# The first stage of an encoder trunk: projections from x * w with rstd at the readout, and all engines in written order

## The chip, the cores and the metric

The kernel runs on one core of a Trainium2 chip. The metric is the device time of one launch in microseconds (us); the median of three runs before is 2257.11 us. TensorE (PE) does the matmuls, VectorE (DVE), ScalarE (ACT) and GpSimd (POOL) the elementwise work; SyncE (SP) and, here and there, ACT issue the transfers (DMAs). PE writes PSUM, eight banks of 128 x 512 fp32; DVE and ACT read and write it too.

## The reference

One encoder layer runs over a prompt of 1024 tokens and a sample of 256 tokens, with a width of 1024, all fp32. The change touches only the beginning of the token-mixing block:

```python
def rmsnorm(x, w):
    y = xf * lax.rsqrt(jnp.mean(xf * xf, -1, keepdims=True) + EPS)
    return y * w
...
h = rmsnorm(x, norm_mix_w)
proj = h @ w_in          # columns: q/k/v, ab, gate, sg_u (512), sg_v (512), two branch gates
...
def spatial_gating_branch(u, v, ln_w, ln_b, w_s, b_s):
    u = gelu(u)
    v = layernorm(gelu(v), ln_w, ln_b)
    mixed = einsum('gts,bnsgc->bntgc', w_s, v) + b_s      # chunks of 128 tokens, 4 groups
    return u * mixed
```

After it come the gated DeltaNet branch, the branch merge, cross-attention into 256 memory tokens, a SwiGLU feed-forward part and a last norm.

## The kernel before

**Tiles.** Tokens lie in three blocks, `BLOCKS`: prompt blocks 0 and 1 of 512 tokens each and block 2, the sample, of 256. x is held with its 1024 features as 8 pieces (k) of 128 partitions and the tokens along the free axis. Every fp32 product is made of three fp32r matmuls: an operand is split into a high part, an ACT copy with rounding, and a low part, source minus high part (`split`: the copy on ACT, the subtraction on the engine that is named). Per k there is hi*hi, lo*hi and hi*lo. So x becomes `hi{b}`, `lo{b}`, and a weight `whi`, `wlo` (or `svh`, `svl` for the v columns).

**Norm.** `Norm.add` squares on ACT and adds on DVE; the rest sums over the partitions with matmuls against a column of ones, computes rstd with 11 small DVE instructions (`rsqrt` has three Newton steps), broadcasts rstd over the partitions by matmuls with the identity, and then, for each k, one DVE instruction makes x * w * rstd (`nt`) and `split` makes its two parts. `to_h` gives the low part to POOL for even k and to DVE for odd k.

**Stages.** The first stage computes, block by block, `sgv(b)` (the v columns in two halves of 264, tokens as the stationary operand, each token group of 128 with 24 matmuls, followed by `gelu2` on ACT and DVE) and `sgu(g, b)` (u group g of 128 columns, 24 matmuls). The order on PE is: sample's v, `bias()`, sample's u groups 0 and 1; block 0's v, u groups 0 and 1; block 1's v, u groups 0 and 1; then u groups 2 and 3 of all blocks. `ln(cs)` is the layer norm of v, and `mix(g, b, ug)` the spatial mix, which writes to DRAM. Behind this stage come the DeltaNet stage with the remaining projections, and the rest of the layer.

**Order of the work.** PE runs in the order in which the program is written (`manual_schedule` for TensorE). All other engines are ordered by a scheduler with its own cost model. Side work is written as generators (`K.side`): each yields an estimate of PE time in ns after which it wants to go on, and `K.pump` lets it go on when PE's estimated clock is there. `K.until` and `K.finish` push the side work on until it is done. `LAG0` and similar numbers are such estimates. Weights stream through a queue, `K.order`: `K.take` hands out the next split weight, `K.ahead` splits one more and loads the next. The low part of a split weight is made by POOL in this stage.

**Start.** SP issues the sample's x (`xs`), the small vectors `sm` (norm weights among them), two constants, half of the v weights, the rest of the constants; then block 0's x (`x0`) and the other half of the v weights. The sample's norm (`first_norm`) runs while the v weights are split, half 0 by POOL and DVE, half 1 likewise.

Of the kernel before, what the change touches and what calls it, by code (L numbers as in the profile page):

```python
# [8 lines left out]
F32 = mybir.dt.float32  # L9
F32R = mybir.dt.float32r  # L10
# [31 lines left out]
def f32(ap):  # L42
    return ap.bitcast(F32)
# [11 lines left out]
class Trunk:  # L55
# [68 lines left out]
    def split(self, hi, lo, src, eng=None):  # L124
        self.nc.scalar.activation(hi, src, AF.Copy)  # L125
        (eng or self.nc.vector).tensor_tensor(out=lo, in0=src, in1=f32(hi), op=ALU.subtract)  # L126
# [37 lines left out]
def trunk_kernel(ctx: ExitStack, tc: tile.TileContext, a):  # L164
# [52 lines left out]
    def bank(p=pq, tag="b"):  # L217
        return p.tile([P, 512], F32, tag=tag, name="bank")
# [4 lines left out]
    def rsqrt(y, x, scratch):  # L223
        V.tensor_scalar(out=y.bitcast(I32), in0=x.bitcast(I32), scalar1=-0.5, scalar2=float(0x5F3759DF), op0=ALU.mult, op1=ALU.add)
        for _ in range(3):
            V.scalar_tensor_tensor(out=scratch, in0=y, scalar=-0.5, in1=x, op0=ALU.mult, op1=ALU.mult)
            V.tensor_tensor(out=scratch, in0=scratch, in1=y, op=ALU.mult)
            V.scalar_tensor_tensor(out=y, in0=scratch, scalar=1.5, in1=y, op0=ALU.add, op1=ALU.mult)

    class Norm:  # L230


# [62 lines left out]
    def to_h(h, b):  # L295
        return lambda k, t: split(h[b][0][:, k, :], h[b][1][:, k, :], t, V if k % 2 else G)

    def act_tiles(p=None):

        p = p or hp  # L300
        return [
            (
                p.tile([P, KT, n], F32R, tag=f"hi{b}", name=f"hi{b}"),
                p.tile([P, KT, n], F32R, tag=f"lo{b}", name=f"lo{b}"),
            )
            for b, (_, n) in enumerate(BLOCKS)
        ]
# [29 lines left out]
            SY.dma_start(x[:, k : k + 2, :], src[:, k : k + 2, t0 : t0 + n])  # L337
        return x

    def sv_raw(half):  # L340
        raws = [K.raw() for _ in range(2)]
        for i, raw in enumerate(raws):
            SY.dma_start(raw, a["w_sv"][half][:, i * 1056 : (i + 1) * 1056])
        return raws

    def sv_split(half, raws):
        lo = svp.tile([P, 8 * 264], F32R, tag="lo", name="svl")
        hi = svp.tile([P, 8 * 264], F32R, tag="hi", name="svh")
        for i, raw in enumerate(raws):
            sl = slice(i * 1056, (i + 1) * 1056)  # L350
            split(hi[:, sl], lo[:, sl], raw, V if i else G)
        sv.append((hi, lo))


    xs = hp.tile([P, KT, NS], F32, tag="lo1", name="xs")
    for k in range(0, KT, 2):
        SY.dma_start(xs[:, k : k + 2, :], a["xT"][:, k : k + 2, NP:])
    SY.dma_start(sm, a["small"])
    SY.dma_start(cst[:, C_BD:], a["const"][:, C_BD:])
    sv_raw0 = sv_raw(0)  # L360
    SY.dma_start(cst[:, :C_BD], a["const"][:, :C_BD])
    x_h = act_tiles()

    def first_norm():

        nm = Norm(xp, 512)
        for k in range(0, KT, 2):
            nm.add(xs[:, k : k + 2, :].rearrange("p k t -> p (k t)"))
        nm.n = NS
        yield from nm.rest(lambda k: xs[:, k, :], S_MIX, to_h(x_h, 2), 0, lag=0, halves=2)  # L370

    first = K.side(first_norm())
    sv_split(0, sv_raw0)
    x0 = x_load(a["xT"], 0, 512, "x0")
    sv_split(1, sv_raw(1))
    K.finish(first)

    done = set()

    def other_norms():  # L380
        yield from norm(xp, lambda k: x0[:, k, :], 512, S_MIX, to_h(x_h, 0), 600, 0, LAG0)
        done.add(0)
        x1_ = x_load(a["xT"], 512, 512, "x1")
        yield 3000
        yield from norm(xp, lambda k: x1_[:, k, :], 512, S_MIX, to_h(x_h, 1), 900)
        done.add(1)
        mem = x_load(a["memT"], 0, 512, "mem")
        yield 6000
        yield from norm(xp, lambda k: mem[:, k, :], 512, S_MEM, lambda k, t: SY.dma_start(md[k], t))

    norms = K.side(other_norms())


    ybd = dp.tile([HEADS, P, NTOK], F32, name="ybd")
# [31 lines left out]
    bias2 = sp.tile([P, 4, P], F32, name="bias2")  # L426
    SY.dma_start(bias2, a["sg_b"].unsqueeze(0).to_broadcast([P, 4, P]))

    def ln(cs):
# [8 lines left out]
        V.tensor_scalar(out=var[:, cs], in0=var[:, cs], scalar1=1.0 / 512, scalar2=4.0 * EPS, op0=ALU.mult, op1=ALU.add)  # L438
# [56 lines left out]
        V.tensor_copy(gcol.rearrange("p d r -> p (d r)"), pt[:, :80])  # L495

    def sgv(b):
        if b < 2:
            K.until(norms, lambda: b in done)
        for half in (0, 1):  # L500
            w = sv[half]
            nv = 264 if half == 0 else 248
            for c in range(4 * b, min(4 * b + 4, NCH)):
                cs = slice((c % 4) * P, (c % 4 + 1) * P)
                hi, lo = x_h[b]
                ps = bank(pm)
                n = 0
                for k in range(KT):
                    wh, wl = wk(w, k, 264)
                    for l, r in ((hi[:, k, cs], wh), (lo[:, k, cs], wh), (hi[:, k, cs], wl)):  # L510
                        mm(ps[:, :264], l, r, n == 0, n == 23)
                        n += 1
                    yield 0
                acc = (s0 if half == 0 else s1)[:, c : c + 1]
                gelu2(sp, ps[:, :nv], vg[:, c, half * 264 : half * 264 + nv], nv, acc)
                if half:
                    V.tensor_copy(ab[:, c, :], ps[:, 248:264])
        lns[b] = K.side(ln(slice(4 * b, min(4 * b + 4, NCH))))
        K.ahead()

    def bias():
# [6 lines left out]
    def mix(g, b, ug):  # L528
# [11 lines left out]
        V.tensor_tensor(out=ug, in0=ug, in1=mx, op=ALU.mult)  # L540
        SY.dma_start(ybd[g, :, t0 : t0 + n], ug)

    ws, mixes = [], []

    def sgu(g, b):
        t0, n = BLOCKS[b]
        if len(ws) == g:
            ws.append(K.take())
        ps = bank(pm)[:, :n]
        yield from proj(ps, ws[g], x_h, b)  # L550
        if (g, b) in ((0, 2), (0, 1), (2, 2), (3, 2)):
            K.ahead()
        if len(mixes) > 2:
            K.finish(mixes[-3])
        ug = sp.tile([P, 512], F32, tag="ug", name="ug", bufs=3)[:, :n]
        gelu2(sp, ps, ug, n)
        mixes.append(K.side(mix(g, b, ug)))

    for b in (2, 0, 1):
        K.main(sgv(b))  # L560
        if b == 2:
            bias()
        elif b == 1:
            K.side(decays())
        K.main(sgu(0, b))
        K.main(sgu(1, b))
# [1564 lines left out]
```

## Time and profile before

| | us |
|---|---|
| median of 3 runs | 2257.11 (2254.49 to 2257.84) |
| the profiled execution | 2255.0 |
| its span, first to last instruction | 2253.2 |
| PE busy | 2196.2 (97%) |
| DVE busy | 1394.0 (62%) |
| ACT busy | 815.5 (36%) |
| POOL busy | 532.7 (24%) |

The page has 40 slices of 56 us each; the first one is the stage that is changed. A line of the timeline begins with the start in us from the begin of the span and the duration; then come the engine, the line of the kernel, the operation, and what it writes and reads. A number in brackets at the end is how long the engine had been idle before, and what ended that. A group's line ends with its busy time, the mean of one in ns, and the idle time before its instructions. Matmuls overlap, so their pace is the distance of their starts and not their duration.

### The profile page before, as it was taken

The numbers are of one execution on the slowest core, as the hardware profiler recorded it, in microseconds if no ns is written. First come the engines' busy times: TensorE is split into PE (matmuls) and PEld (weight loads), VectorE is DVE, ScalarE is ACT, GpSimd is POOL, SyncE is SP. The second block draws the span as 40 slices with busy tenths as digits, with TensorE's granted clock in tenths as the row PEclk, the third lists the DMA queues.
The fourth block names the chain that finished last, engine by engine and source line by source line (L and its number), as shares of the span: only waits on it lengthen the run. The fifth ranks groups of instructions, "written<-read, shape, count | busy, mean of one in ns | idle before, by whom it ended". The sixth has DMA issues, their size and how long they took to land.

```text
span 2253.2 us, 32407 instructions
## 1 busy us (share of the span) xinstructions
PE 2196.2 (97%) x12468; PEld 1918.3 (85%) x12468; DVE 1394.0 (62%) x2770; ACT 815.5 (36%) x1481; POOL 532.7 (24%) x355
## 2 busy tenths in 40 slices
PE   6999999999999999999999999899999999999998
PEld 6988888888888898888888888688888888888888
DVE  7768788887985964664534537544334334568575
ACT  5434243433424433233343423323232323243453
POOL 3010000000000000013231331565666566300031
PEclk9999999999999999999999999999999999999999
DMA  5221322223234445962231431223222222493531
GB/s 185 83 79 68 104 69 87 77 69 95 73 111 125 159 140 165 305 236 94 84 106 45 157 143 57 75 76 110 87 82 76 88 76 82 136 363 126 198 111 57
DMA packets 191301, 262.47 MB, mean 116 GB/s; under 512 B 72410, under 2 KB 102698, under 8 KB 191146
## 3 DMA queue, kind: packets, MB, share of 16 engines
q1 hardware_dynamic: 171306, 231.30, 30.9%
q10 hardware_dynamic: 19840, 29.11, 3.5%
q8 instruction: 97, 1.59, 0.3%
q14 instruction: 58, 0.48, 0.1%
HBM read 182.19 MB, written 78.16 MB: 116 GB/s over the span
## 4 chain that ended last, share of the span: by engine, by line
PE 82%; DVE 8%; issue 4%; DMA 2%; ACT 2%; POOL 1%; SPq 0%; POOLq 0%; ACTq 0%; DVEq 0%
PE bank L108 81%; PE bank L121 1%; DMA tbd<-stage 1%; DVE acc L599 1%; DVE wlo L126 1%; DMA t<-sgd 1%; DVE nt L284 1%; DVE U L845 0%; DVE sw L903 0%; DVE lo L126 0%; DMA stage<-gtd 0%; DVE W L745 0%; DVE nacc L249 0%; DVE aT L714 0%; DVE zt L837 0%
## 5 line engine op out<-in xcount | busy, mean ns | idle before, releaser
L108 PE MATMUL bank<-hi,whi 128*128 128x512 f32 (+1 forms) x2144 | 763.3, 356 | 2.8 <-ACT whi L125 1.7
L108 PE MATMUL bank<-lo,whi 128*128 128x512 f32 (+1 forms) x2144 | 748.8, 349 | 1.1 <-POOL lo L126 1.1
L108 PE MATMUL bank<-hi,wlo 128*128 128x512 f32 (+1 forms) x2144 | 748.3, 349 | 0.9 <-DVE wlo L126 0.9
L108 PEld LDWEIGHTS bank<-hi,wlo 128*128 128x128 f32 x2144 | 406.0, 189 | 54.9 <-DVE wlo L126 1.3
L108 PEld LDWEIGHTS bank<-hi,whi 128*128 128x128 f32 x2144 | 406.9, 190 | 52.7 <-ACT whi L125 2.2
L108 PEld LDWEIGHTS bank<-lo,whi 128*128 128x128 f32 x2144 | 407.1, 190 | 49.8 <-POOL lo L126 1.4
L126 POOL TENSOR_TENSOR wlo<-raw,whi 128x1024 fp32r<-128x1024 f32 x70 | 177.8, 2542 | 377.2 <-ACT whi L125 377.2
L125 ACT ACTIVATE whi<-raw 128x1024 fp32r<-128x1024 f32 (+1 forms) x141 | 144.5, 1026 | 195.3 <-PE bank L108 146.9
L126 POOL TENSOR_TENSOR wlo<-room,whi 128x1024 fp32r<-128x1024 f32 x42 | 100.6, 2396 | 115.7 <-ACT whi L125 115.7
L108 PE MATMUL bank<-bhl,whi 128*128 128x512 f32 x408 | 125.7, 389 | 0.0
L126 DVE TENSOR_TENSOR wlo<-raw,whi 128x1024 fp32r<-128x1024 f32 (+1 forms) x71 | 82.3, 1159 | 43.6 <-ACT whi L125 41.5
L125 ACT ACTIVATE whi<-room 128x1024 fp32r<-128x1024 f32 x42 | 44.6, 1061 | 142.5 <-PE bank L108 138.6
L1796 DVE TENSOR_TENSOR room<-room,bank 128x512 f32<-128x512 f32 x21 | 14.5, 688 | 131.8 <-ACT room L1567 131.8
L108 PEld LDWEIGHTS bank<-bhl,whi 128*128 128x128 f32 x408 | 76.5, 188 | 15.9
L599 DVE SCALAR_TENSOR_TENSOR acc<-craw,sm,acc 128x510 f32<-128x510 f32 (+1 forms) x96 | 73.6, 766 | 20.5 <-ACT acc L597 19.0
L108 PE MATMUL bank<-bhl,wlo 128*128 128x512 f32 x204 | 79.5, 390 | 1.2 <-DVE wlo L126 1.2
L745 DVE TENSOR_TENSOR W<-W,UT 128x2 f32<-128x2 f32 (+30 forms) x155 | 73.2, 472 | 10.1 <-DMA W<-in_eye 5.8
L248 ACT ACTIVATE nsq<-x 128x512 f32<-128x512 f32 (+1 forms) x70 | 40.2, 583 | 102.7 <-DVE x L1237 92.4
L962 ACT ACTIVATE gs<-bank 128x512 f32<-128x512 f32 (+1 forms) x60 | 31.2, 520 | 125.2 <-PE bank L108 119.9
L1589 DVE SCALAR_TENSOR_TENSOR t<-bank,t 128x512 f32<-128x512 f32 (+1 forms) x44 | 24.6, 558 | 82.2 <-PE bank L108 82.2
L249 DVE TENSOR_TENSOR nacc<-nacc,nsq 128x512 f32<-128x512 f32 (+1 forms) x72 | 54.4, 755 | 33.2 <-ACT nsq L248 31.9
L108 PE MATMUL bank<-bhl,ahl 128*128 128x512 f32 x312 | 73.8, 392 | 0.0
(345 smaller groups left out, 4223.1 us busy)
## 6 DMA issues: line engine op xcount, KB each, us to landing
raw<-in_w_gu SPq DMA_DIRECT2D x44, 512.0 KB, 3.9
braw<-gq SPq DMA_DIRECT2D x14, 1024.0 KB, 5.4
raw<-in_w_g SPq DMA_DIRECT2D x20, 512.0 KB, 3.3
gq<-t SPq DMA_DIRECT2D x33, 256.0 KB, 2.0
gtd<-gs ACTq DMA_DIRECT2D x32, 256.0 KB, 2.0
w<-in_w_dn SPq DMA_DIRECT2D x8, 1024.0 KB, 11.9
raw<-in_w_qkv SPq DMA_DIRECT2D x12, 512.0 KB, 3.6
gq<-r SPq DMA_DIRECT2D x22, 256.0 KB, 4.3
```

The costliest lines, as they stand in the source:

```text
L108: self.nc.tensor.matmul(out, l, r, start=start, stop=stop, skip_group_check=more)
L121: self.nc.tensor.transpose(out, x, ident)
L125: self.nc.scalar.activation(hi, src, AF.Copy)
L126: (eng or self.nc.vector).tensor_tensor(out=lo, in0=src, in1=f32(hi), op=ALU.subtract)
L248: S.activation(sq, x, AF.Square)
L249: (eng or V).tensor_tensor(out=self.acc, in0=self.acc, in1=sq, op=ALU.add)
L284: V.scalar_tensor_tensor(out=t, in0=xk(k), scalar=sm[:, wcol + k : wcol + k + 1], in1=pb[:, :n], op0=ALU.mult, op1=ALU.mult)
L599: V.scalar_tensor_tensor(out=dst, in0=src, scalar=wj, in1=dst, op0=ALU.mult, op1=ALU.add)
L745: V.tensor_tensor(out=t3, in0=u3[:, i:, c:].rearrange("p j c -> p c j"), in1=XL[:, 32 * i + i : 32 * i + 32].unsqueeze(1).to_broadcast([P, ...
L962: S.activation(t, ps, AF.Tanh, scale=0.5)
L1589: V.scalar_tensor_tensor(out=out, in0=u, scalar=sign, in1=t, op0=ALU.mult, op1=ALU.mult)
L1796: V.tensor_tensor(out=c22, in0=c22, in1=pe, op=ALU.add)
```

## The change

The stage's beginning, until block 0's x is normalised, is written out by hand and put under `manual_schedule` for DVE, ACT, POOL and SP as well, so that each engine runs it in the order of the text.

- The sample's v and u (groups 0 and 1) are computed from x * w (`xw`, split by ACT's scaled copy and one DVE instruction) in place of the normalised x. rstd comes in when the product is read: for v as the per-token scale of ACT's square and tanh and, since the layer norm that follows takes a common factor out, in its epsilon (`e2`); for u by a multiply with rstd broadcast over the partitions (`rb2`).
- rstd itself is computed by `rsqrt9`, 8 instructions in place of 10.
- The v weights are split by ACT and DVE alone. POOL gets only the low parts of the first two u weights and of half of block 0's x.
- `sm` and two constants are issued by ACT; the order of SP's transfers is new, and the remaining constants come last.
- Block 0's squares are made between the sample's steps, with sums in PSUM.
- `sgv(0)` takes token groups 0 to 2 together in half 0, so that each k gives nine matmuls in place of three.
- The sample's normalised x (`hi2`, `lo2`), needed by u groups 2 and 3 and the later projections, is made afterwards in `other_norms`, ahead of block 1's norm.

```diff
-    def sv_split(half, raws):
-        ...
-            split(hi[:, sl], lo[:, sl], raw, V if i else G)
...
-        yield from nm.rest(lambda k: xs[:, k, :], S_MIX, to_h(x_h, 2), 0, lag=0, halves=2)
...
+    first_stage.enter_context(tc.manual_schedule(engines={V.engine, S.engine, G.engine, SY.engine}))
...
+    S.dma_start(sm, a["small"])
+    S.dma_start(cst[:, C_BD:], a["const"][:, C_BD:])
+    S.dma_start(ident, a["const"][:, C_ID : C_ID + P])
+    xs_load(0)
+    sv_load(0, 0)
+    for k in (2, 4, 6):
+        xs_load(k)
+    sv_load(0, 1)
+    for i in range(2):
+        sv_load(1, i)
+    SY.dma_start(raw_u[0], a["w_u"][0])
     x0 = x_load(a["xT"], 0, 512, "x0")
+    SY.dma_start(raw_u[1], a["w_u"][1])
...
     def sgv(b):
...
+        for half, cs in ((0, (0, 1, 2)), (0, (3,)), (1, (0,)), ...) if b == 0 else [(half, (c,)) for half in (0, 1) for c in range(4)]:
...
+    def xw_split(*ks):
+        w = lambda k: sm[:, S_MIX + k : S_MIX + k + 1]
+        for k in ks:
+            S.activation(xw[:, 0, k, :], xs[:, k, :], AF.Copy, scale=w(k))
+        for k in ks:
+            V.scalar_tensor_tensor(out=xw[:, 1, k, :], in0=xs[:, k, :], scalar=w(k), in1=f32(xw[:, 0, k, :]), op0=ALU.mult, op1=ALU.subtract)
...
+    xw_split(0, 1)
+    square2(0)
+    sv_split(0, 0)
+    xw_split(2, 3)
+    xw_split(4, 5)
+    xw_split(6, 7)
+    sv_split(0, 1)
+    for k in (2, 4, 6):
+        square2(k)
+    sv_split(1, 0)
+    for k0 in (0, 4):
+        for i in range(2):
+            sgv2(0, k0, i)
...
+    rsqrt9(y2, ms, sc, e2)
...
+    sv_split(1, 1)
+    K.split_w(0)
+    square0(0, 1)
+    gelus = [gelu_pair(half) for half in range(2)]
+    next(gelus[0])
+    square0(2, 3)
+    for _ in gelus[0]:
+        pass
+    sgv2(1, 0, 0)
+    sgv2(1, 0, 1)
+    sgv2(1, 4, 0)
...
+    sgv2(1, 4, 1)
+    rb2 = raw_u[0][:, :NS]
+    S.activation(rb2, pb2[:, :NS], AF.Copy)
+    square0(4, 5)
+    next(gelus[1])
+    K.split_w(1)
+    square0(6, 7)
+    for _ in gelus[1]:
+        pass
+    pu = sgu2(0, range(KT))
+    ugs = [sgu2_out(0, pu)]
+    pu = sgu2(1, range(4))
...
+    rsqrt9(y0, ms, sc, h0)
+    sgu2(1, range(4, 8), pu)
+    ugs.append(sgu2_out(1, pu))
...
+    bias()
...
+    for k in range(KT):
+        t = sq_tile()
+        V.scalar_tensor_tensor(out=t, in0=x0[:, k, :], scalar=sm[:, S_MIX + k : S_MIX + k + 1], in1=pb0, op0=ALU.mult, op1=ALU.mult)
+        to_h(x_h, 0)(k, t)
+    first_stage.close()
...
+    def other_norms():
+        x1_ = x_load(a["xT"], 512, 512, "x1")
+        yield NORM2
+        for k in range(KT):
+            ...
+            to_h(x_h, 2)(k, t)
+            yield 600
+        x_h[1] = ...
+        yield from norm(xp, lambda k: x1_[:, k, :], 512, S_MIX, to_h(x_h, 1), 900)
...
-        if (g, b) in ((0, 2), (0, 1), (2, 2), (3, 2)):
+        if (g, b) in ((0, 1), (2, 2), (3, 2)):
             K.ahead()
...
-    for b in (2, 0, 1):
+    for b in (0, 1):
         K.main(sgv(b))
...
-LAG0, LAGF, LAGF2, PACEF = 7500, (8000, 6000, 1500), (9000, 9000, 2800), 1000
+NORM2, LAGF, LAGF2, PACEF = 4000, (8000, 6000, 1500), (9000, 9000, 2800), 1000
```

More of the change, by code (lines that the diff above doesn't have):

```diff
@@ new lines, in square0, with sgv2 @@
+    def square0(*ks):
+        ts_ = {}
+        for k in ks:
+            ts_[k] = sq_tile() if k else accp
+            S.activation(ts_[k], x0[:, k, :], AF.Square)
+        for k in ks:
+            if k:
+                V.tensor_tensor(out=accp if k < KT - 1 else acc0, in0=accp, in1=ts_[k], op=ALU.add)
+    def sgv2(half, k0, i):
+        for k in range(k0, k0 + 4):
+            w = wk(sv[half], k, 264)[i]
+            for x in range(2 - i):
+                for c in range(2):
+                    mm(ps2[half][c][:, :264], xw[:, x, k, c * P : (c + 1) * P], w, i + x + k == 0, i == 1 and k == KT - 1)
@@ new lines, in trunk_kernel @@
+    sgv2(1, 4, 1)
[6 more added lines that the diff above has]
+    for _ in gelus[1]:
+        pass
+    pu = sgu2(0, range(KT))
+    ugs = [sgu2_out(0, pu)]
+    pu = sgu2(1, range(4))
+    pc0 = bank()
+    for c in range(4):
+        mm(pc0[:, c : c + 1], acc0[:, c * P : (c + 1) * P], one)
+    ms, sc = pc0[:, 4:8], pc0[:, 8:12]
+    V.tensor_scalar(out=ms, in0=pc0[:, :4], scalar1=C9 / D, scalar2=C9 * EPS, op0=ALU.mult, op1=ALU.add)
@@ L545, in sgu @@
+    norms = K.side(other_norms())
+    for g in range(2):
+        mixes.append(K.side(mix(g, 2, ugs[g])))
     def sgu(g, b):
```

174 lines of the change are left out of this document (115 added, 59 removed).

## The prediction

> **What bounds the kernel now.** I read the page first, then the stretches of the first 56 us, then the timeline of TensorE (PE) until the second prompt block begins, and last the groups of VectorE (DVE) and ScalarE (ACT) in these stretches.
>
> ```profile
> span 2253.2 us, 32407 instructions
> PE 82%; DVE 8%; issue 4%; DMA 2%; ACT 2%; POOL 1%; SPq 0%; POOLq 0%; ACTq 0%; DVEq 0%
> ...
> 0.00:20.00 20.00, 7.11 (x27) 6.12 (x28) 10.69 (x27) 9.29 (x16) 5.10 (x9) 1.00 0.89 307
> 20.00:40.00 20.00, 16.98 (x116) 15.81 (x116) 16.07 (x43) 11.30 (x22) 8.10 (x4) 0.91 0.28 105
> 40.00:56.00 16.00, 13.45 (x81) 11.97 (x80) 14.61 (x34) 9.89 (x21) 6.00 (x4) 0.79 0.36 130
> ```
>
> The chain of waits is PE for 82% of the span: the kernel is PE's stream of matmuls, and only holes in it can be won. The stretches (columns: length, then busy time of PE, its weight loads, DVE, ACT, POOL, then granted clock, DMA share, GB/s) show where the holes are: PE is busy 7.1 of the first 20 us, 17.0 of the next 20 and 13.5 of the next 16, and in the third stretch the clock was 0.79. The change touches just this part. The holes in detail:
>
> ```profile
> 15.37 0.59 PE L108 MATMUL bank<-svh,hi 128*128 128x264 f32 x1 [1.54 <-ACT hi L125]
> ...
> 19.08 0.42 PE L108 MATMUL bank<-svh,lo 128*128 128x264 f32 x1
> ...
> 20.18 0.42 PE L108 MATMUL bank<-svh,hi 128*128 128x264 f32 x1
> ...
> 21.30 0.28 PE L108 MATMUL bank<-svh,hi 128*128 128x264 f32 x1
> ```
> ```profile
> 44.01 0.29 PE L108 MATMUL bank<-svh,hi 128*128 128x264 f32 x1
> ...
> 46.10 0.39 PE L108 MATMUL bank<-svh,lo 128*128 128x264 f32 x1 [0.73 <-DVE lo L126]
> ...
> 51.24 0.59 PE L108 MATMUL bank<-svh,lo 128*128 128x264 f32 x1
> ```
> ```profile
> 76.47 0.40 PE L108 MATMUL bank<-hi,whi 128*128 128x512 f32 x1
> ...
> 87.36 0.28 PE L108 MATMUL bank<-svh,hi 128*128 128x264 f32 x1
> ...
> 88.57 0.28 PE L108 MATMUL bank<-svh,lo 128*128 128x264 f32 x1
> ```
>
> The first projection starts at 15.37 (its x needs the whole norm first). From 19.08 to 20.18 lie five matmuls, 0.22 us each; from 87.36 to 88.57 ten, 0.121 each. So matmuls run at half rate for some 5.9 us after the first one, until 21.30, and again after the stalls of 45 to 51 us. The sample's v half and two u groups end at 44.01. The v projection of prompt block 0 (192 matmuls, 23.2 us at 0.121) then takes until 76.47, 32.5 us. The broadcast, the statistics and two small mixes inside it account for some 2.4 us:
>
> ```profile
> 64.85 0.95 PE L108 MATMUL bank<-cst,nacc 128*128 128x1 f32 x8
> ...
> 69.01 1.09 PE L108 MATMUL bank<-cst,nst 128*128 128x128 f32 x8
> ```
>
> (0.80 and 0.85 until the next matmul starts, and the mixes, four 128-column matmuls each, at an estimated 0.37 by the second row.) So 32.5 - 23.2 - 2.4 = 6.9 us of it is waiting and half rate. Two groups of u matmuls (48, 10.9 us) follow to 87.36, where block 1's v starts. **87.36 is my landmark**: behind it PE's work is the same in both kernels, so the gain is what this start moves, if nothing is given back.
>
> **Part by part. (1) The start.** The sample's v and u now multiply x*w; rstd is applied when PSUM is read. The first matmul waits for x*w and a weight half, not for the norm.
>
> ```profile
> 2.00:3.00 1.00, 0.00 (x0) 0.00 (x0) 0.00 (x0) 0.01 (x1) 0.00 (x0) 1.00 0.94 289
> ...
> 11.00:12.00 1.00, 0.00 (x0) 0.00 (x0) 0.83 (x6) 0.90 (x1) 1.00 (x1) 1.00 1.04 401
> ```
> ```profile
> 3.54 0.63 ACT L245 ACTIVATE nacc<-xs 128x512 f32<-128x512 f32 x1 [1.53 <-DMA xs<-in_xT]
> ...
> 6.87 0.17 DVE L405 TENSOR_SCALAR h<-sm 128x9 f32<-128x9 f32 x1 [0.99 <-DMA sm<-in_small]
> ...
> 10.40 0.17 DVE L266 TENSOR_SCALAR bank<-bank 128x2 f32<-128x2 f32 x1 [1.96 <-PE bank L108]
> ...
> 12.39 0.16 DVE L228 SCALAR_TENSOR_TENSOR nst<-bank,nst 128x2 f32<-128x2 f32 x1
> ```
>
> The sample's x rows arrive at 289 GB/s, weights at 401. The first 262 KB of x were there at 3.54; the small vectors, behind all of x on SP's queue, only at 6.87. They now go out on ACT's queue beside the first piece, with the identity: 384 KB together, 0.4 us more, so ACT's first scaled copy starts at about 4.2. Behind it in written order:
>
> ```profile
> L125 ACT ACTIVATE svh<-raw 128x1056 fp32r<-128x1056 f32 x4 | 4.3, 1075 | 2.7 <-DMA raw<-in_w_sv 2.7
> L125 ACT ACTIVATE hi<-nt 128x256 fp32r<-128x256 f32 x8 | 3.2, 413 | 4.5 <-DVE nt L284 4.5
> ...
> L248 ACT ACTIVATE nsq<-x 128x512 f32<-128x512 f32 x9 | 5.3, 621 | 0.4 <-DMA x<-in_xT 0.3 <-POOL lo L126 0.2
> ```
>
> ACT: two copies (0.8), a square (0.6), the first weight piece (1.08), for which 541 KB at 401 GB/s arrive by about 5.6: first matmul at 6.7. All of ACT's list (8 copies 3.3, 4 squares 2.5, 4 pieces 4.3) and about 0.6 us of waiting for transfers end near 14.4, after small overlaps. DVE takes over all low parts, two weight pieces that POOL did included:
>
> ```profile
> 17.97 0.42 DVE L126 TENSOR_TENSOR lo<-nt,hi 128x256 fp32r<-128x256 f32 x1
> ...
> 27.77 1.25 DVE L126 TENSOR_TENSOR svl<-raw,svh 128x1056 fp32r<-128x1056 f32 x1
> ```
>
> 8 x 0.42, 3 x 1.25 and three adds of 0.62 keep it on ACT's heels to 15.0. PE has 48 matmuls: 6.7 to some 15.0 with its half-rate start, and the sample's statistics are ready at 15.5. The second half follows at once and ends at 21.8. The new rsqrt is 8 instructions for 10; in the old chain 11 took 10.40 to 12.55, 0.195 each, so rstd and its two by-products end at 17.6.
>
> **(2) DVE in written order from 17.6.** This engine sets when block 0's x is scaled. Durations, with the groups of 60 to 112 us:
>
> ```profile
> L249 DVE TENSOR_TENSOR nacc<-nacc,nsq 128x512 f32<-128x512 f32 x11 | 7.6, 687 | 0.1
> L284 DVE SCALAR_TENSOR_TENSOR nt<-x,sm,bank 128x512 f32<-128x512 f32 x8 | 5.8, 746 | 1.3 <-issue 1.3
> ...
> L126 DVE TENSOR_TENSOR lo<-nt,hi 128x512 fp32r<-128x512 f32 x4 | 2.8, 690 | 0.0
> L411 DVE SCALAR_TENSOR_TENSOR gt<-gt,bank 128x264 f32<-128x264 f32 x6 | 2.6, 428 | 2.3 <-ACT gt L410 2.3
> ```
>
> One starts about 0.07 before its predecessor's end, so I count 0.62, 0.66, 0.62 and 0.36. Last weight piece 1.2; block 0's seven adds 4.4 (they go to PSUM, which no row shows: 0.62 by the add, 0.66 by the scale that reads PSUM, 0.3 us in all; I take the lower as it is the same instruction); eight gelu steps 3.0; two small copies 0.3; waits for ACT's squares and tanh 0.6: 27.1. Then u group 0's readout (three steps of 0.36, three crossings to ACT, 2.15), block 0's rsqrt (9 x 0.2), u group 1's readout (2.15, its multiply by rstd included), the bias (1.5): 34.7. DVE stands still in these crossings, and what is queued behind it is block 0's x. PE has nothing left at 31.7. POOL's low half of u group 1 (its raw piece lands near 20: 1.2 MB ahead of it at 289 GB/s, 4.8 MB and itself at 401; ACT reaches it at 23) ends at 26.6 by this row, 2.4 each, and holds PE from 25.0:
>
> ```profile
> 33.56 4.71 POOL L126 TENSOR_TENSOR wlo<-raw,whi 128x1024 fp32r<-128x1024 f32 x2 [6.27 <-ACT whi L125]
> ```
>
> That is covered: PE is waited for again only at 29.3, by block 0's statistics.
>
> **(3) Block 0.** Per pair of k, DVE does two scales (1.32), waits for ACT's copy (0.70), then one low half (0.62): 2.65, 10.6 in all, 34.7 to 45.3. Before, the same went from 38.81 to 51.18, mixed with other work:
>
> ```profile
> 38.81 2.06 DVE L284 SCALAR_TENSOR_TENSOR nt<-x,sm,bank 128x512 f32<-128x512 f32 x3 [0.39 <-PE bank L108]
> ...
> 50.49 0.69 DVE L126 TENSOR_TENSOR lo<-nt,hi 128x512 fp32r<-128x512 f32 x1
> ```
>
> PE's first low half comes from POOL at 37.6. With three token groups a pair gives PE 18 matmuls, 2.2 us at full rate or 4 at half rate; it starts at half rate after about 6 us of rest, 41.6 after the first pair, then stays just behind DVE: three groups done at 48.2, the other 120 matmuls and the 2.4 us of small ones at 65.1, u of block 0 until **76.0** against 87.36. That splits into an earlier start (44.0 to 37.6, 6.4) and waiting of 1.9 instead of 6.9 (5.0).
>
> **(4) What is late next.** The sample's normalised x, skipped at first, is made now (for u groups 2 and 3 far behind). DVE must do this from 45.3 until block 1's x is ready: 8 v readouts (6.8), the sample's layer norm (3.8), the sample's 8 scales and 4 low halves (4.6), 7 adds for block 1 (4.3), its rsqrt (2.2), 8 scales and 4 low halves (7.8), two mixes (1.6): 31.1, u's first gelu outside. In 40:56, the stretch where PE waited on it, DVE was busy 14.61 of 16, 91%: 31.1/0.91 = 34.2, to 79.5. PE can begin block 1's v 2.5 us ahead of the last k (its first 24 matmuls take 2.9), thus at 77.0; one u gelu (1.3) falls into it: 78.3. **Gain 87.36 - 78.3 = 9.0 us.**
>
> The rest costs nothing: the removed weight split after u(0,2) is done by the explicit splits; the remaining constants, moved behind the weights, are needed only by the decays behind block 1; w_u[2]'s load on SP waits on buffers freed by 12. The profiled execution took 2255.0 (span 2253.2): 2246.0. The median is 2.1 higher, 2257.1: **2248.1**.
>
> **Rivals.** A measurement of this kernel tells 0.2%, 4.5 us, from no change.
>
> *PE-bound (0.10).* DVE fits its list in; block 1 starts at 76.0 or a little earlier: gain 11.4 or more, 2245.7. For: DVE was ahead before, with block 1's last low half, against PE at 87.36:
>
> ```profile
> 80.04 0.69 DVE L126 TENSOR_TENSOR lo<-nt,hi 128x512 fp32r<-128x512 f32 x1
> ```
>
> Against: 31 us of work in 31 us.
>
> *Port contention in block 0 (0.20).* A DVE instruction with SBUF operands waits for POOL's:
>
> ```profile
> 47.89 1.26 DVE L224 TENSOR_SCALAR sums<-sums 128x2 int32<-128x2 int32 x1
> ```
>
> A two-element instruction took 1.26, 0.16 alone. If each odd low half waits for POOL's even one (1.4), a pair is 3.4, the loop 3 us longer: gain 6.0, 2251.1. Against: low halves of 0.69 beside POOL's in the groups above. The Trainium skill, Advanced Engine Details and Errata, VectorE Performance Modes, states that the second Vector port is shared with GpSimd and that the two block each other. By that rule this rival holds; the row of 1.26 agrees, the group of 690 ns doesn't for this instruction.
>
> *Given back (0.08).* The other engines' order later is not written by hand; a new wait of 7 us there: 2255.
>
> *DVE becomes the bound (0.14, slower).* The same contention all along: the loop ends at 48.3, and the list runs at the 67% of the first 40 us (10.69 + 16.07 of 40): 46.4, to 94.7, block 1 starts at 92.2, 4.9 late, 2262.0. It decides from 74%, where 31.1 us need 42. For: both engines are in written order and stand still at every crossing. Against: 91% under pressure.
>
> **How the numbers follow.** Forecast 0.48, with 2245 to 2251 of its own; the rivals as given. Faster by over 0.2% (below 2252.6): 0.48 + 0.10 + 0.15 of the port rival = 0.73. Slower: 0.14. Within: 0.13. The range 2243 to 2257.5 leaves out the slower case and a little at the low end.
>
> **What would show it.** Right: first v matmul near 6.7; DVE's first block-0 scale near 34.7 with PE idle some 6 us before it; u of block 0 starting near 65; block 1's v near 78, released by DVE's low halves. Wrong: block 0's scales after 38.8, pairs over 3.2 us, or block 1's v at 84 or later; or these in place and the span not 9 shorter, which would put the loss behind 130 us.

## The result and the profile after

The change made the kernel slower: 2262.81 us median of 11 runs (2260.63 to 2269.31) against 2257.11 of before, ratio 1.0031 [1.0022, 1.0039], about 7 us (the two medians lie 5.7 apart). The profiled execution took 2260.63, its span is 2258.8. The forecast was 2248.1, so the sign was wrong. The first line of the page after and its chain of waits, then the stretches (columns as above):

```profile
span 2258.8 us, 32415 instructions
PE 79%; DVE 10%; issue 4%; DMA 3%; ACT 2%; POOL 1%; SPq 0%; ACTq 0%; POOLq 0%; DVEq 0%
```
```profile
0.00:20.00 20.00, 12.26 (x80) 12.26 (x81) 11.49 (x27) 13.48 (x23) 2.73 (x5) 1.00 0.90 330
20.00:40.00 20.00, 14.34 (x97) 12.91 (x96) 16.43 (x50) 11.04 (x25) 3.65 (x2) 0.91 0.24 95
40.00:56.00 16.00, 13.27 (x85) 12.03 (x86) 14.50 (x29) 6.60 (x16) 6.08 (x6) 0.89 0.30 102
...
80.00:100.00 20.00, 16.20 (x98) 15.11 (x97) 17.59 (x38) 12.39 (x27) 3.07 (x2) 0.83 0.33 119
...
130.00:168.00 38.00, 34.65 (x183) 29.90 (x182) 19.74 (x40) 8.40 (x15) 4.87 (x6) 0.91 0.18 64
```

The same two late stretches in the kernel before:

```profile
80.00:100.00 20.00, 20.00 (x137) 18.43 (x136) 15.87 (x42) 11.79 (x27) 0.00 (x0) 1.00 0.35 132
...
130.00:168.00 38.00, 37.56 (x206) 32.26 (x207) 20.69 (x40) 9.05 (x15) 2.54 (x6) 1.00 0.21 78
```

The early stretch did win: PE was busy 12.26 of the first 20 us in place of 7.11. But behind 80 us, where PE had been full at a clock of 1.00, it now has holes and a clock of 0.83 and 0.91, and DVE has 2 points more of the chain of waits. PE's timeline after shows where:

```profile
7.74 1.47 PE L108 MATMUL bank<-svh,xw 128*128 128x264 f32 x5 [7.74 <-ACT svh L125]
...
38.66 0.39 PE L108 MATMUL bank<-svh,hi 128*128 128x264 f32 x1 [3.25 <-ACT hi L125]
...
48.00 0.39 PE L108 MATMUL bank<-svh,lo 128*128 128x264 f32 x1 [1.18 <-POOL lo L126]
...
71.99 0.40 PE L108 MATMUL bank<-hi,whi 128*128 128x512 f32 x1
...
83.81 0.28 PE L108 MATMUL bank<-svh,hi 128*128 128x264 f32 x1
...
90.21 2.16 PE L108 MATMUL bank<-sw,vg 128*128 128x128 f32 x8 [3.17 <-DVE vg L445]
...
117.47 0.40 PE L108 MATMUL bank<-hi,whi 128*128 128x512 f32 x1
...
134.28 2.17 PE L108 MATMUL bank<-sw,vg 128*128 128x128 f32 x8 [3.03 <-DVE vg L445]
...
138.83 0.63 PE L108 MATMUL bank<-hi,whi 128*128 128x512 f32 x1
...
169.25 0.48 PE L108 MATMUL bank<-hi,whi 128*128 128x512 f32 x1
```

The rows of before that answer to 117.47, 138.83 and 169.25 (block 1's u, the next 512-wide matmul behind the decays, and the first one behind the last sixteen mix matmuls, which I call the **stage's last row**):

```profile
115.21 0.40 PE L108 MATMUL bank<-hi,whi 128*128 128x512 f32 x1
...
133.25 0.39 PE L108 MATMUL bank<-hi,whi 128*128 128x512 f32 x1
...
163.34 0.48 PE L108 MATMUL bank<-hi,whi 128*128 128x512 f32 x1
```

Block 1's v starts 3.55 us earlier (83.81 for 87.36). From there to block 1's u it takes 33.66 in place of 27.85, 5.8 lost: a wait of 3.17 for the layer norm's `vg` ahead of a mix, one of 0.64 for a low half, and half rate behind them. From there to the 512-wide row it takes 21.36 in place of 18.04, 3.3 lost: 3.03 waiting for `vg` again. 3.55 - 5.8 - 3.3 = -5.6, as much as the spans of these two executions differ (2258.8 - 2253.2); at 169.25 the kernel is 5.9 behind. So the whole of the loss lies between 84 and 139 us, in matmuls that the change doesn't touch.

On DVE and POOL the block-0 loop looks like this (two timelines; L688 are the scales, L226 and L445 belong to the sample's layer norm, L433 to block 0's, L700 to the sample's second normalisation):

```profile
37.21 1.40 DVE L688 SCALAR_TENSOR_TENSOR nsq<-x,sm,bank 128x512 f32<-128x512 f32 x2
...
38.72 1.26 DVE L226 SCALAR_TENSOR_TENSOR sums<-sums 128x2 f32<-128x2 f32 x1
...
46.28 1.94 DVE L445 TENSOR_SCALAR vg<-vg,sums 128x512 f32<-128x512 f32 x2
...
51.71 0.95 DVE L700 SCALAR_TENSOR_TENSOR nsq<-xs,sm 128x256 f32<-128x256 f32 x1 [1.18 <-POOL lo L126]
52.58 1.01 DVE L126 TENSOR_TENSOR lo<-nsq,hi 128x512 fp32r<-128x512 f32 x2
...
77.24 1.27 DVE L433 TENSOR_SCALAR sums<-sums 128x4 f32<-128x4 f32 x1
```
```profile
38.68 1.27 POOL L126 TENSOR_TENSOR lo<-nsq,hi 128x512 fp32r<-128x512 f32 x1 [10.41 <-ACT hi L125]
...
46.45 1.49 POOL L126 TENSOR_TENSOR lo<-nsq,hi 128x512 fp32r<-128x512 f32 x1 [2.61 <-ACT hi L125]
...
75.46 3.03 POOL L126 TENSOR_TENSOR lo<-nt,hi 128x512 fp32r<-128x512 f32 x2 [15.11 <-ACT hi L125]
```

The loop takes 16.0 us (37.21 to 53.26; the row at 52.58 holds block 0's last low half, 0.68, and one of the sample's). In it stands the sample's layer norm, which the scheduler has put there: two-element instructions, 0.16 us otherwise. The first one that begins behind POOL's low half ends only with it and takes 1.26 us (38.72 behind 38.68), and what is queued behind it on DVE, block 0's own low half, is late by as much. In the fourth pair two scales of the sample's second normalisation stand too, the second behind a wait of 1.18 for POOL.

The same hold lies inside PE's two waits for `vg`. On the way to the `vg` of 90.21 a four-element instruction of block 0's layer norm takes 1.25, and on the way to that of 134.28 one of block 1's takes 2.20, beside a low half of a weight. DVE, then POOL:

```profile
86.40 1.25 DVE L226 SCALAR_TENSOR_TENSOR sums<-sums 128x4 f32<-128x4 f32 x1
...
130.86 2.20 DVE L228 SCALAR_TENSOR_TENSOR sums<-sums 128x4 f32<-128x4 f32 x1
```
```profile
85.88 1.76 POOL L126 TENSOR_TENSOR lo<-nt,hi 128x512 fp32r<-128x512 f32 x1 [1.42 <-ACT hi L125]
...
130.70 2.34 POOL L126 TENSOR_TENSOR wlo<-raw,whi 128x1024 fp32r<-128x1024 f32 x1 [3.84 <-ACT whi L125]
```

So some 2 of the 3.03 us at 134.28 are an instruction held by POOL (an estimate: 2.20 less 0.16).

### The profile page after: what moved, and what is told of

Its sections match the earlier page's. It is cut to its first block, busy times and chain, and to the rows that moved or that the text cites. A ratio compares the mean times of both kernels' runs of the same rounds, so it can differ in the third digit from the quotient of the medians.

```text
span 2258.8 us, 32415 instructions
## 1 busy us (share of the span) xinstructions
PE 2200.2 (97%) x12468; PEld 1922.8 (85%) x12468; DVE 1404.0 (62%) x2780; ACT 818.1 (36%) x1490; POOL 527.2 (23%) x353
## 4 chain that ended last, share of the span: by engine, by line
PE 79%; DVE 10%; issue 4%; DMA 3%; ACT 2%; POOL 1%; SPq 0%; ACTq 0%; POOLq 0%; DVEq 0%
PE bank L108 78%; PE bank L121 1%; DMA tbd<-stage 1%; DVE acc L766 1%; DVE wlo L126 1%; DVE W L912 1%; DVE lo L126 0%; DVE sw L1070 0%; DVE nacc L262 0%; DVE W L915 0%; DVE nt L297 0%; DMA braw<-gq 0%; DVE U L1012 0%; DMA stage<-gtd 0%; ACT whi L125 0%
## 5 line engine op out<-in xcount | busy, mean ns | idle before, releaser
L912 DVE TENSOR_TENSOR W<-W,UT 128x2 f32<-128x2 f32 (+30 forms) x155 | 73.1, 472 | 10.6 <-DMA W<-in_eye 6.3
L1404 DVE SCALAR_TENSOR_TENSOR x<-bank,x 128x512 f32<-128x512 f32 (+1 forms) x48 | 28.6, 598 | 70.0 <-PE bank L108 64.1
```

The lines of the kernel that those rows point to most:

```text
L912: V.tensor_tensor(out=t3, in0=u3[:, i:, c:].rearrange("p j c -> p c j"), in1=XL[:, 32 * i + i : 32 * i + 32].unsqueeze(1).to_broadcast([P, ...
L1404: V.scalar_tensor_tensor(out=x[b][:, m, :], in0=ps, scalar=scale, in1=x[b][:, m, :], op0=ALU.mult, op1=ALU.add)
```

## The experiments

e1 to e16 ran in five rounds beside the kernel before, whose medians there were 2254.6 to 2255.7 (2257.11 beside the change itself); us against before are the ratio's. "Block 1's v" and "last row" are rows of each profile.

| run | block 1's v | last row | ratio | us against before |
|---|---|---|---|---|
| before | 87.36 | 163.34 | 1 | 0 |
| after | 83.81 | 169.25 | 1.0031 [1.0022, 1.0039] | +7.0 |
| e1 mixes later | 84.18 | 166.17 | 1.0016 [1.0008, 1.0025] | +3.6 |
| e2 block 0 without POOL | 80.00 | 164.12 | 1.0018 [1.0009, 1.0027] | +4.1 |
| e3 one norm | 81.00 | 164.29 | 1.0006 [0.9997, 1.0015] | +1.4 |
| e5 groups one at a time | 90.02 | 174.05 | 1.0053 [1.0041, 1.0065] | +12.0 |
| e6 side chain early | 89.12 | 171.71 | 1.0023 [1.0013, 1.0032] | +5.2 |
| e7 sample's norm last | 82.33 | 165.95 | 1.0009 [1.0000, 1.0018] | +2.0 |
| e8 = e7, e2, table early | 77.98 | 163.31 | 0.9992 [0.9983, 1.0000] | -1.8 |
| e9 = e8, block 1 without POOL | 77.93 | 161.04 | 0.9985 [0.9976, 0.9995] | -3.4 |
| e10 = e9, e1 | 77.03 | 156.87 | 0.9981 [0.9972, 0.9989] | -4.3 |
| e11 = e9, weights without POOL | 76.84 | 157.33 | 0.9973 [0.9964, 0.9982] | -6.1 |
| e12 = e9 with both | 76.92 | 154.52 | 0.9971 [0.9961, 0.9982] | -6.5 |
| e13 before, weights without POOL | 87.30 | 162.11 | 1.0003 [0.9994, 1.0012] | +0.7 |
| e14 before, with both | 85.58 | 158.85 | 0.9990 [0.9980, 1.0001] | -2.3 |
| e15 = e12, sample's norm first | 79.24 | 159.87 | 0.9994 [0.9982, 1.0006] | -1.4 |
| e16 = e12, POOL in blocks 0 and 1 | 79.77 | 160.25 | 0.9980 [0.9970, 0.9990] | -4.5 |

Executions of one kernel spread over 4 to 13 us, and the rows are those of one. It lay from 5.3 us below its kernel's median (e12, the fastest of its seven; e9's was 2.7 above) to 7.0 above (e6); rows and ratios differ by up to 3.3 us. Where two intervals overlap, as those of the change and of e1, e2 or e6, their difference is likely and not settled.

**e1: the mixes later.** Theory: what is lost is a wait of place; PE, in written order, meets a mix before DVE's layer norm is through.

```diff
-        yield MIX
+        yield MIX + (4000 if g < 2 and b < 2 else 0)
```

> The changed kernel with one number changed: the spatial mixes of u groups 0 and 1 of both prompt blocks stand 4 us of PE's estimated time later in PE's written order. Theory 'place' (DVE is not short of time; PE meets the mixes too early): PE's waits of 3.2 us near 90 and 3.0 us near 134, and the half rate behind them, go: 5 to 8 us faster than the changed kernel, 2255 to 2258 us. Theory 'DVE bound' (DVE is late as a whole, whatever stands behind it waits as well): the waits show up elsewhere, at most 2 us faster, 2261 us or more.

The wait of 3.17 is gone and 3.4 us come back, but smaller waits for block 1's low halves and the next consumer take part of its place:

```profile
131.52 0.63 PE L108 MATMUL bank<-cst,gm 128*40 128x128 f32 x4 [2.77 <-DVE gm L484]
```

The gain lies between what the two theories expected. So place is likely a real part, and DVE is late as well, not only the mixes early.

**e2: block 0's low halves all on DVE, each a step behind its scale.**

```diff
-        to_h(x_h, 0)(k, t)
+        if k:
+            split(hi0[:, k - 1, :], lo0[:, k - 1, :], last_t, V)
+        last_t = t
+    split(hi0[:, KT - 1, :], lo0[:, KT - 1, :], last_t, V)
```

> The changed kernel with block 0's eight low halves all on DVE, each one step behind its scale, so that POOL does not run beside DVE in that loop. Theory 'port' (DVE instructions blocked while POOL runs): the loop shrinks from 16.4 us to 11 to 12, block 0's u starts near 68 instead of 72, and the total is 4 to 6 us lower, 2257 to 2259 us. Theory 'work' (DVE simply has more to do than PE allows): 2.5 us more DVE work, no gain or 1 to 3 us slower, 2263 to 2266 us.

```profile
35.24 1.40 DVE L688 SCALAR_TENSOR_TENSOR nsq<-x,sm,bank 128x512 f32<-128x512 f32 x2
...
45.31 0.69 DVE L126 TENSOR_TENSOR lo<-nsq,hi 128x512 fp32r<-128x512 f32 x1
```

With four low halves more for DVE the loop is shorter: 10.8 us, 35.24 to 46.00. The edit does two things, though. POOL is out of the loop, and as each low half stands a step behind its scale, DVE no longer waits for ACT's copy. In those waits the scheduler had put the layer norm, which now stands behind the loop but for two small instructions. What each of the two is worth isn't separated. Block 1's v comes 3.8 us earlier than after, and 2.9 us of it reach the end, less than the 4 to 6 expected: the waits for `vg` behind it are still there (3.15 and 3.03).

**e3: no second normalisation.** `xw` is kept in `hi2`, `lo2`; left out is rstd in the sample's u groups 2 and 3 and its later projections.

```diff
         yield NORM2
-        for k in range(KT):
-            ...
-            to_h(x_h, 2)(k, t)
-            yield 600
+        yield 4800
```

> The changed kernel without the sample's second normalisation: its later projections take x * w as it is, so rstd is left out there. 8 scales, 8 copies and 8 low halves are gone (4 on DVE, 4 on POOL). Theory 'work': DVE is 5 to 6 us ahead from 54 us on, block 1's v doesn't wait: 4 to 6 us faster than the changed kernel, 2257 to 2259 us. Theory 'place': the positions on PE stay, at most 1 us faster. If the port alone is the cause: 1 to 2 us, for the low halves on POOL.

5.6 us come back: the same time as before within the interval. The sample's second normalisation is the costliest of the parts of the change that were left out or put back alone. But it isn't the whole of it, for waits of 1.93 and 3.03 remain.

**e5: block 0's token groups one at a time.**

```diff
-        for half, cs in ((0, (0, 1, 2)), (0, (3,)), (1, (0,)), ...) if b == 0 else [(half, (c,)) for half in (0, 1) for c in range(4)]:
+        for half, cs in [(half, (c,)) for half in (0, 1) for c in range(4)]:
```

> The changed kernel with block 0's token groups one at a time again. My prediction's working: the three groups hide block 0's scaling; without them PE waits for the last k near 53.6 and has 168 matmuls (20.3 us) left: block 0's u near 76 instead of 72, the total 4 us higher, 2266 to 2267 us. Theory 'DVE bound': DVE sets when block 1 can start, so PE's four us are lost in a wait that is there anyway: 0 to 2 us higher, 2263 to 2265 us.

5.0 us slower than the change, as the prediction's working has it: three groups taken together are worth some 5 us here.

**e6: the side chain early** (NORM2 from 4000 to 1000, its step from 600 to 200).

> The changed kernel with shorter pauses in the side work: NORM2 1000 instead of 4000, 200 instead of 600 per k of the sample's second normalisation, so that block 1's statistics, rstd broadcast and the memory's norm stand about 3.4 us earlier in PE's order; the work is the same. Theory 'position' (the norms stand too close ahead of their users): PE's waits at the mixes shrink, 3 to 5 us faster than the changed kernel, 2257 to 2260 us at 2256 for before. Theory 'DVE bound': PE then waits some 4 us for block 1's sums at the statistics, no gain, 2261 to 2264 us.

1.8 us faster, which the overlapping intervals don't tell from no gain. The wait moves to the statistics' `nacc` (3.05 at 65.37), as the second theory has it: with the same work and shorter pauses block 1's sums come 3.1 us sooner (68.48 after), but PE asks for them sooner still. Its profiled execution was 7 us over its median and is read for the place of the wait alone.

**e7: the second normalisation behind block 1's norm,** made from the split x * w. NORM2 goes from 4000 to 6000, and the pauses ahead of block 1's norm are 6000 in all in place of 8800.

```diff
         yield NORM2
+        x_h[1] = ...
+        yield from norm(xp, lambda k: x1_[:, k, :], 512, S_MIX, to_h(x_h, 1), 900)
+        done.add(1)
+        ...
         for k in range(KT):
-            V.scalar_tensor_tensor(out=t, in0=xs[:, k, :], ..., in1=rb2, ...)
+            V.tensor_tensor(out=t, in0=f32(xwp[0][:, k, :]), in1=f32(xwp[1][:, k, :]), op=ALU.add)
+            V.tensor_tensor(out=t, in0=t, in1=pbs[:, :NS], op=ALU.mult)
             to_h(x_h, 2)(k, t)
-        ...
-        done.add(1)
+        done.add(2)
```

> The changed kernel with the sample's second normalisation moved behind block 1's norm (made from the split x * w, which needs one more DVE instruction per k, and 2 broadcast matmuls). Theory 'order' (the second normalisation stands between block 0 and block 1's norm and delays DVE and the position by 4 to 5 us): block 1's v finds its x ready, the wait near 90 goes or is under 1 us, 4 to 7 us faster, 2256 to 2259 us. Theory 'work' (DVE has too much in total until 130 us): 2.9 us more DVE work, the wait at the later mixes grows, 0 to 2 us faster, 2261 us or more.

It costs DVE one more instruction for each k and is still 5 us faster than the change: what cost time was where that work stood, ahead of block 1's norm, for shorter pauses alone brought no such gain (e6). But the wait for `vg`, which by the theory goes or falls under 1 us, is still 2.94 (at 87.25), and one of 2.97 for `gm` stands at 130.81.

**e8 and e9: parts together.** e8 is e7 with e2, and an activation on two elements ahead of everything, so that ACT's table is loaded before x arrives; e9 also makes block 1's low halves on DVE.

```diff
+    V.memset(beta[:, 0, :2], 1.0)
+    S.activation(beta[:, 0, :2], beta[:, 0, :2], AF.Square)
...
-        yield from norm(xp, lambda k: x1_[:, k, :], 512, S_MIX, to_h(x_h, 1), 900)
+        yield from norm(xp, ..., lambda k, t: split(x_h[1][0][:, k, :], x_h[1][1][:, k, :], t, V), 900)
```

> As the last one, and block 0's low halves all on DVE one step behind their scale, and an activation on a small tile right behind ACT's transfers so that its table is loaded before x arrives. If the causes add (order 4 to 7, port 3, table 1.3): 8 to 11 us faster than the changed kernel, 2251 to 2255 us, at or below before. If they are one and the same lack of DVE time: 4 to 6 us, 2257 to 2259 us.

> As the last one, with block 1's low halves all on DVE too: 4 low halves (2.5 us) more on DVE, but no POOL beside it. Theory 'port': block 1's scaling takes 11 us instead of 15, 1 to 3 us faster than the last one. Theory 'work': 0 to 2 us slower than it.

In e8 the first matmul starts at 6.54 and block 1's v at 77.98; it is 8.8 us faster than the change, as it should be if the causes add. e9 is the first version whose interval lies below 1. What its own edit brings isn't settled: 1.6 us by the ratios, while the medians of e8 and e9 are the same. PE's rows of e9:

```profile
77.93 0.28 PE L108 MATMUL bank<-svh,hi 128*128 128x264 f32 x1
...
81.72 0.94 PE L108 MATMUL bank<-sw,vg 128*128 128x128 f32 x4 [1.82 <-DVE vg L447]
...
84.28 0.42 PE L108 MATMUL bank<-svh,lo 128*128 128x264 f32 x1
84.50 0.42 PE L108 MATMUL bank<-svl,hi 128*128 128x264 f32 x1
...
125.73 0.63 PE L108 MATMUL bank<-cst,gm 128*40 128x128 f32 x4 [3.03 <-DVE gm L486]
```

Block 1's v is 9.4 us ahead of before, yet the last row only 2.3: with block 1's v where the prediction has it, 7 us are given back behind it.

**e10 to e12: what gives it back.** e10 adds e1's edit to e9; e11 sets `K.lo_vector = True` behind the start, so that DVE makes the weights' low halves; e12 has both.

> The version with the sample's second normalisation behind block 1's, the table loaded early and the low halves of blocks 0 and 1 on DVE (2253.9), with the small mixes of u groups 0 and 1 of the prompt blocks set 4 us of PE time later. Theory PLACE (PE meets the mix before DVE's layer norm is done; what it loses is the wait and the half rate behind it): the waits of 1.8 at 81.7 and 3.0 at 125.7 are gone or under 0.7, the 512-wide matmuls behind block 1's u start at 127 to 129 in place of 130.7, 2 to 4 us faster than that version, 2250 to 2252. Rival DVE-BOUND (DVE's list is too long, so any later matmul that needs it waits as well): the waits move to the next low half or to the decays, gain under 1 us, 2253 to 2254.5.

> The same version with the low halves of all weights behind the first stage's start made by DVE in place of POOL (until the point where the kernel does so anyway). Theory PORT (DVE's small instructions for layer norm and decays are held about 2 us each while POOL makes a weight's low half of 2.4 us): the wait for gm of 3.0 at 125.7 shrinks to under 1.5, 1 to 3 us faster, 2251 to 2253, although DVE then does some 1.2 us more for every weight. Rival WORK (DVE has no room for them): gm waits as long or longer, 0 to 2 us slower, 2254 to 2256.

> Both edits of the two runs before: mixes 4 us later and low halves of the weights on DVE. If waits of place and of port are separate costs they add: 4 to 6 us faster than the version without them, 2248 to 2250. If either one alone removes the same wait, no more than the better of the two, 2250 to 2252.

e10's wait at the mix is gone, as PLACE has it, but that for `gm` is not (2.89) and one of 1.54 for `nacc` has come (99.25); what it gains is 4.2 us by the last row and 0.9 by the ratio. e11 gains 3.7 and 2.7. In e9 a decay instruction of 128 x 80 lay under POOL's low half of a weight; in e11 the same one takes 0.23. DVE and POOL of e9, then DVE of e11:

```profile
117.34 2.09 DVE L476 TENSOR_TENSOR wk<-wk 128x80 f32<-128x80 f32 x1
```
```profile
116.92 2.41 POOL L126 TENSOR_TENSOR wlo<-raw,whi 128x1024 fp32r<-128x1024 f32 x1 [26.99 <-ACT whi L125]
```
```profile
117.39 0.23 DVE L476 TENSOR_TENSOR wk<-wk 128x80 f32<-128x80 f32 x1
```

e12 beats both kernels, by 6.5 us against before. Its last row, at 154.52, is 8.8 ahead of before, but in an execution that was 5.3 us faster than its kernel's median:

```profile
76.92 0.28 PE L108 MATMUL bank<-svh,hi 128*128 128x264 f32 x1
...
106.46 0.40 PE L108 MATMUL bank<-hi,whi 128*128 128x512 f32 x1
...
121.41 0.63 PE L108 MATMUL bank<-cst,gm 128*40 128x128 f32 x4 [2.11 <-DVE gm L486]
...
154.52 0.48 PE L108 MATMUL bank<-hi,whi 128*128 128x512 f32 x1
```

The wait for `gm` shrank from 3.03 to 2.11 and didn't go, so e11's number for it (under 1.5) was missed: it is 2.28 there. Whether both edits add can't be told from the ratios of e11 and e12.

**e13 and e14: the same repairs in the kernel before.** e13 sets `K.lo_vector` ahead of block 0, e14 has e1's edit too.

> Control: the kernel before, with the low halves of the later weights (from u groups 2 and 3 on) made by DVE in place of POOL. Theory PORT as a cost that the kernel before pays too: its wait of 1.3 at 130.35 goes, 0.5 to 2 us faster than before, 2253.7 to 2255.2. If the port costs only where DVE is behind PE, as after the change: the same as before within 0.5 us.

> Control: the kernel before with both repairs of the last version that fit it, the mixes of u groups 0 and 1 set 4 us later and the low halves of the later weights on DVE. If the repairs only take back what the change lost: the same as before, within 1 us, and the row behind 161.64 at most 1.5 us earlier. If the kernel before has the same losses: 3 us or more faster than before, and only about half of the 6.5 us between before and the last version belong to the change of the start.

e13 changes nothing in time: its wait of 1.3 at 130.35 is gone and one of 0.97 for `gr` has come. e14 gains 2.3 us by the ratio, whose interval still reaches 1, and 4.5 by the last row, between what the two theories expected. So the kernel before likely pays a part of these costs too, and of e12's 6.5 us some 4 belong to the changed start with its repairs (6.5 - 2.3 by the ratios, 158.85 - 154.52 = 4.3 by the rows; the intervals of the two just touch).

**e15 and e16: e12 with one thing put back,** the second normalisation ahead of block 1's norm, or the even low halves of blocks 0 and 1 on POOL.

> The last version with the sample's second normalisation back ahead of block 1's norm, all else kept (table, low halves of blocks 0 and 1 and of the weights on DVE, later mixes). If the place of the second normalisation is a cost of its own: 3 to 5 us slower than the last version, 2252.5 to 2254.5, with a wait of 1 us or more at block 1's v or its statistics. If it cost only because DVE was held up elsewhere: within 1.5 us of it, 2249.5 to 2251.

> The last version with the even low halves of blocks 0 and 1 back on POOL, all else kept. Theory PORT: block 0's loop is about 16 us again in place of 10.7, block 1's v starts at 82 in place of 77, and the version is 3 to 5 us slower, 2252.5 to 2254.5. If the time is set elsewhere by now: less than 1.5 us slower, though the loop is longer.

e15 is 5.2 us slower than e12 by the ratio and 5.4 by the row, with waits of 2.32 at 52.85 and 1.79 at 84.06, and the two intervals meet only at 0.9982: the place of that work, with the pauses that go with it, is a cost of its own, also where POOL is out of the way. In e16 the loop is 14.9 us again (34.43 to 49.33; 10.5 in e12) and block 1's v 2.9 later. At the last row it is 5.7 us later, but only 2 us slower by the ratio, short of the 3 to 5 expected and with an interval that overlaps e12's, so its price in time isn't settled. The hold is plain, in the same layer-norm instruction of e16 and of e12:

```profile
35.94 1.27 DVE L226 SCALAR_TENSOR_TENSOR sums<-sums 128x2 f32<-128x2 f32 x1
```
```profile
44.03 0.15 DVE L226 SCALAR_TENSOR_TENSOR sums<-sums 128x2 f32<-128x2 f32 x1
```

The layer norm stands in different places: in e16 it fills the waits of the loop, in e12 it stands behind the loop but for two instructions. With loop and layer norm together DVE is through at 49.33 in e16 and at 48.84 in e12. So what ends 4 us sooner is block 0's x, and not DVE's work as a whole.

## Why the prediction was wrong, step by step

- **The start was right, 1 us short.** Predicted 6.7, measured 7.74. The missing us is mostly ACT's table load. Before, it ran while x was on its way; now three DMA issues stand ahead of it on ACT, and it waits behind the first activation's transfer. ACT's rows of before and of after:

```profile
0.73 1.28 ACT L245 ACT_TABLE_LOAD   x1 [0.73 <-PEq L2119]
```
```profile
3.99 1.28 ACT L556 ACT_TABLE_LOAD   x1 [3.99 <-DMA xs<-in_xT]
```

  With the table loaded early (e8) it is 6.54. The trace of before held the row; the working did not count it as moved.
- **DVE's written list was nearly right.** The first scale was forecast at 34.7 and came at 37.21: 1.6 later at its beginning (rstd and its by-products at 19.2 for 17.6), and 18.0 in place of 17.1 long. Executions differ here: it lies at 35.24 to 37.32 in those with the start as changed, and at 34.43 (e12) to 35.99 in those with the table early. PE's rest ahead of block 0 was 3.25, not 6, for its last work there (second u group, bias, rstd's broadcast) ended later (35.4 for 31.7).
- **The block-0 loop was mis-sized:** 16.0 us for 10.6, pairs of 3.87 for 2.65, just what the text named as a sign that it is wrong (over 3.2). The port rival held that price (3.4) and set it aside on the group of 690 ns. That was a misreading: those low halves had begun ahead of POOL's or beside none, and then it is POOL's that takes longer (before: 1.59 at 73.34 in place of 1.30, behind a low half of DVE begun at 73.10). One that began behind POOL's took 1.23 (e16, 48.10). And what is held here is mostly not the low half but the scheduler's other work, which the working had not placed in the loop at all: 1.1 us each in the first two pairs (1.26 and 1.28 for 0.16), some 0.9 in the third (1.94 for the 1.00 of e12 at 47.84), and in the fourth the sample's scales with the wait of 1.18. Without both, POOL's halves and most of that work, it is 10.8 (e2). The Trainium skill, SBUF — State Buffer, "Who interferes with whom", states that a DVE instruction with two SBUF inputs contends with a GpSimd instruction that reads SBUF, and that the later one waits until the first is done; the runs agree (1.27 against 0.15, e16 and e12). A TENSOR_SCALAR with one input was held as well (1.27 at 77.24), which that sentence doesn't cover. The sentence of the Trainium skill that the prediction cites (Advanced Engine Details and Errata, VectorE Performance Modes) says it of GpSimd and of Vector instructions in 2-port modes, a condition that the prediction left out.
- **What is late next was nearly right in length:** from the loop's end to block 1's last low half forecast 34.2 us, measured 36.4 (53.26 to 89.69). So block 1's v stood at 83.81 for 78.3: gain 3.55 of 9.0.
- **The step that failed** was "behind it PE's work is the same in both kernels, so the gain is what this start moves", with the rest put at nothing. PE's work is the same; when its suppliers are ready is not. The sample's second normalisation was counted for block 1's v alone, but it pushes block 1's and the memory's norm, and with them the layer norms and decays, back on DVE: the broadcast of block 1's rstd stands 11.1 us ahead of block 1's v after (72.68 to 83.81), 18.35 before (69.01 to 87.36). PE, earlier, then met two mixes that DVE had not got to, and the two stretches took 5.8 and 3.3 us more; small layer-norm instructions held beside POOL (1.25 and 2.20) are part of it. The rival "given back" named this place and 7 us (measured: 9.1) and got 0.08. What took the sign was this step more than the loop: with the loop at its forecast length (e2) block 1's v is 7.4 us ahead of before and the kernel still 4.1 slower, and e9 has block 1's v where it was forecast (77.93) and still loses 7 us behind it. With the waits eased e12 is 6.5 us faster; that its last row shows nearly the forecast 9 (8.8) is partly luck, for it comes from an execution 5.3 us under its kernel's median, and the repairs of e10 and e11 alone move before's last row by 4.5 (e14).
- **PE-bound and DVE-bound** did not happen as told. Block 1's v was not late (83.81, not 92.2), but DVE is the bound in short stretches all along. That the DVE-bound rival's time, 2262.0, lies near the measured 2262.81 is luck: it came by another path.
- **The three token groups** were counted right: without them e5 loses 5.0, and the working's 18 matmuls a pair keep PE just behind DVE (e12: u of block 0 at 65.55, forecast 65.1).
- **Open:** how the shortfall divides. Against the forecast 14.7 us were missing; alone e1 gave back 3.4, e2 2.9 and e7 5.0, and e12, which holds them with the table and the low halves of block 1 and of the weights, 13.5 (7.0 + 6.5). What each is worth beside the others is settled for the second normalisation's place (e15), not for POOL (e16) nor for e10 against e11. In block 0's loop POOL and the scheduler's filling were only ever removed together.

## What to carry to other kernels

When a start is moved ahead on an engine that runs in written order, list for the next stages what each supplier must have ready by when: the gain lasts only as far as the slowest of them has slack. Work that is skipped at first and made up later has a place as well as a price, and behind the next block's chain it cost 5 us less than ahead of it, with more instructions. And an engine that helps out can cost more than it gives where it holds the critical one, and so can other work that a scheduler puts into the waits: with POOL's halves on DVE and no waits to fill, a loop of 16.0 us took 10.8.

## What the runs showed of the hardware

- A two-element DVE instruction takes 0.16 us alone and 1.26 to 1.28 beside POOL's low half of 128 x 512; a decay of 128 x 80 took 2.09 beside a low half of 128 x 1024. In these rows it ends within 0.1 us of POOL's instruction, so the price is what is left of that one.
- A short wait of PE may or may not cost half rate. The 1.82 and 0.39 of e9 at 81.7 were followed by matmuls 0.22 apart (84.28, 84.50) until 87; in e15 a wait of 2.32 was followed by matmuls at full rate, 0.12 apart:

```profile
52.85 0.39 PE L108 MATMUL bank<-svh,hi 128*128 128x264 f32 x1 [2.32 <-DVE vg L409]
...
53.08 0.28 PE L108 MATMUL bank<-svh,lo 128*128 128x264 f32 x1
53.20 0.28 PE L108 MATMUL bank<-svl,hi 128*128 128x264 f32 x1
```

  So the wait's length alone does not set its price; what else does was not tried.
- ACT's table load of 1.28 us is free while nothing has arrived (0.73, before), and on the path once it stands behind the first transfer's wait (3.99, after).
